# Moving the eight activation homes of a one-core diffusion-step kernel from one phase modulo 512 bytes to eight

## The chip, the cores and the metric

The kernel runs on one core of one Trainium2 chip. The metric is the device time of one execution in microseconds (us). Three executions of the kernel before took 2007.27, 2007.70 and 2008.75 us; the median is 2007.7 us.

## What is computed

One layer of a hybrid backbone runs over 128 context tokens and 256 latent tokens, 384 in all, with a model width of 2048 and a hidden width of 8192, in fp32:

```
mod = SiLU(cond) @ w_ada + b_ada           -> shift1, scale1, gate1, shift2, scale2, gate2
h   = RMSNorm(x)*(1+scale1)+shift1
proj = h @ w_in                            -> gated DeltaNet (8 heads) and mLSTM (4 heads), both directions
x  += gate1 * RMSNorm(concat(heads) @ w_out)
h   = RMSNorm(x)*(1+scale2)+shift2
x  += gate2 * RMSNorm(relu(h @ w_ffn1)^2 @ w_ffn2)
```

Returned are the new x of both token sets and the final states of the context.

## The kernel before

Each large product is made from three products in the one-pass fp32 type (`F32R`). A weight chunk of 256 rows by 512 columns is loaded by SyncE's DMA queue into a tile `raw` (five of them). ScalarE rounds it into `whi` (line 332) and VectorE subtracts to get the remainder `wlo` (line 333), two buffers each. The activations are kept transposed (features on the partitions, 384 tokens along the row) and split the same way into a high and a low part. `gemm` (from line 337) then issues, for each 128 rows of the contraction, three matmuls into one bank:

- feature-major (`fm=True`, lines 356 to 358): the stationary operand is a slice of `whi` or `wlo`, and the moving operand is 384 tokens of an activation tile;
- token-major (`fm=False`, lines 360 to 362): the stationary operand is 128 tokens of an activation tile, and the moving operand is 512 columns of `whi` or `wlo`.

So each of these matmuls reads one activation tile and one weight tile. TensorE loads a stationary operand for each matmul (the profile's PEld), beside the matmul before.

The activation tiles live in eight homes of 128 partitions by 8 x 384 x 4 = 12,288 bytes. Four are in the pool `hp` under the tags `h00`, `h01`, `h10`, `h11` (high and low part of features 0 to 1023 and of 1024 to 2047). They hold the mixer's input `h` (`alloc_act`, line 314), then the mixer's output `y` (line 1259), then the FFN's input `h`, and at the very end four weight tiles (line 1172). Four are in the pool `fp` under the tags `ah` and `al`, two buffers each (lines 1140 and 1141). They hold the squared-ReLU activations of one 1024-wide block of the hidden layer, and for a time also the broadcast gate rows `gp1` and `gp2` (lines 1073 and 1185) and two weight tiles (line 1099).

The stages run in this order: projections for the mLSTM (`phase1`, to about 296 us), mLSTM heads, DeltaNet quarters (`delta_qk`, `delta_v`, `delta_quarter`), output projection (`mid`, to about 925 us) and the FFN (`ffn`: eight rounds of `up`, feature-major, and `down`, token-major, to about 1972 us), then `final`. Small products for `mod` (line 190) are filled in between. The order on each engine is the program's order with priorities; no cost depends on an address. All waits are derived from which instruction reads and writes which part of which tile.

The pools are laid out one behind the other along a partition's row. The first, `cp` (constants), begins with an unused tile `padc` of 88 x 4 = 352 bytes (line 1222); with it, `hp` begins at byte 8,704 = 17 x 512. A home is 24 x 512 bytes, so the four homes of `hp` and the weight pool `wp` behind them all begin at a multiple of 512. The pool `fp` begins with an unused tile of 192 bytes (line 1267) and its large tiles, too, stand at multiples of 512: three tiles `x1`, the four homes and three tiles `y2`, with the small ones behind. A slice of a home starts at a multiple of 1,536 bytes (feature block) or of 512 bytes (128 tokens) inside it, and a slice of `whi` at a multiple of 512, so both operands of every such matmul start at a multiple of 512.

Some other matmul operands stand elsewhere. The split gate weights `wgh` and `wgl` (line 435, one-pass type, 96 columns, rows of 384 bytes) start 224 bytes past a multiple of 512. The mLSTM values `vaug` (line 689, plain fp32, rows of 257 x 4 = 1,028 bytes per head) start at 480, 0 and 32 bytes past one for the three token tiles, and the states `cn` at 192.

Of the kernel before, what the change touches and what calls it, by code (L numbers as in the profile page):

```python
# [12 lines left out]
F32 = mybir.dt.float32  # L13
F32R = mybir.dt.float32r
# [7 lines left out]
P = 128  # L22
# [3 lines left out]
TOK = NT * P  # L26
# [228 lines left out]
def ada_later(S, sec, nvec=0):  # L255

    for i in range(2):
        if i < 2 - nvec:
            S.todo.append(ada_steps(S, [(sec, 1024 * i + 256 * u) for u in range(4)], 256))
        else:  # L260
            S.todo.extend(ada_vec(S, sec, 1024 * i + 512 * h) for h in range(2))


def gate_step(S, i):
    gate_rows(S, i)
    yield
# [44 lines left out]
    return d  # L311


def alloc_act(S):

    hh = [[S.hp.tile([P, 8, TOK], F32R, tag=f"h{a}{b}", name=f"h{a}{b}") for b in range(2)] for a in range(2)]
    return lambda kt: (hh[kt // 8][0][:, kt % 8, :], hh[kt // 8][1][:, kt % 8, :])


# [63 lines left out]
def wcols(w, c0, n=512, kn=2):  # L383
    return lambda kc: [w[kc * kn * P:(kc + 1) * kn * P, c0:c0 + n]]
# [357 lines left out]
def delta_static(S):  # L742
    nc, dl = S.nc, S.dl
    S.Tm = [dl.tile([P, 6, P], F32, name=f"Tm{d}", bufs=1) for d in range(2)]
    S.Nc = dl.tile([P, 6, 64], F32, name="Nc", bufs=1)
    S.tA = dl.tile([P, 13, 32], F32, name="tA", bufs=1)
    S.X = dl.tile([NI, 32, 32], F32, name="X", bufs=1)
    for t in S.Tm + [S.Nc, S.tA]:
        nc.gpsimd.memset(t, 0.0)
# [379 lines left out]
def ffn(S):  # L1129
    nc, tc, A, c = S.nc, S.tc, S.A, S.c  # L1130
    fp = S.fp
    y2 = [fp.tile([P, D], F32, tag=f"y2_{t}", name=f"y2_{t}") for t in range(NT)]
    w1, w2 = A.w_ffn1[0], A.w_ffn2[0]
    NC = FFN // 1024
    psum_dn = lambda s: S.pm.tile([P, 512], F32, tag="m", name="ps_dn")
    act = {}
    gp2 = []

    def up(ch):
        hi = fp.tile([P, 8, TOK], F32R, tag="ah", name="ah", bufs=2)  # L1140
        lo = fp.tile([P, 8, TOK], F32R, tag="al", name="al", bufs=2)

        def evac(s, ps, b):
            i = 4 * b + s
            rl = fp.tile([P, TOK], F32, tag="rl", name="rl", bufs=3)
            nc.scalar.activation(rl, ps[:, 0:TOK], AF.Relu)
            nc.scalar.activation(hi[:, i, :], rl, AF.Square)  # L1147
            nc.gpsimd.tensor_tensor(rl, rl, rl, op=ALU.mult)  # L1148
            nc.vector.tensor_tensor(lo[:, i, :], rl, hi[:, i, :].bitcast(F32), op=ALU.subtract)
        for b in range(2):  # L1150
            gemm(S, True, wcols(w1, ch * 1024 + b * 512), range(8), S.hT, lambda s, ps, b=b: evac(s, ps, b))
        act[ch] = lambda kt: (hi[:, kt, :], lo[:, kt, :])

    ss = fp.tile([P, NT, 4], F32, name="ssf")

    def down(ch):
        def evac(s, ps, n):
            dst = y2[s][:, n * 512:n * 512 + 512]
            if ch == 0:
                nc.scalar.copy(dst, ps)  # L1160
            else:
                nc.vector.tensor_tensor(dst, ps, dst, op=ALU.add)
            if ch == NC - 1:
                junk = fp.tile([P, 512], F32, tag="fj", name="fj", bufs=2)
                nc.scalar.activation(junk, dst, AF.Square, accum_out=ss[:, s, n:n + 1])
                eng = nc.vector if n == 3 else nc.gpsimd
                g = gp2[min(s, 1)][:, n * 512:n * 512 + 512]
                eng.tensor_tensor(g if s != 1 and n == 3 else dst, dst, g, op=ALU.mult)
        for n in range(4):
            room = ()  # L1170
            if ch == NC - 1 and n == 3:
                t = [S.hp.tile([P, 2, 512], F32R, tag=f"h{a}{b}", name=f"w{a}{b}") for a in range(2) for b in range(2)]
                room = [None, None, t[0:2], t[2:4]]
            gemm(S, False, lambda kp, n=n: [w2[ch * 1024 + kp * 256:ch * 1024 + (kp + 1) * 256, n * 512:n * 512 + 512]],
                 range(4), act[ch], lambda s, ps, n=n: evac(s, ps, n), psum_dn, room=room)

    S.rate = 0.0
    up(0)
    S.rate = R3
    for ch in range(NC):  # L1180
        if ch + 1 < NC:
            up(ch + 1)
        if ch == NC - 1:
            for v in range(2):
                g = fp.tile([P, D], F32, tag=("ah", "al")[v], name=f"gp2_{v}", bufs=2)
                nc.sync.dma_start(g, S.gpd[1][v].partition_broadcast(P))
                gp2.append(g)
        down(ch)
    return y2, ss, gp2
# [17 lines left out]
def body(tc, A, O):  # L1207
    with ExitStack() as ctx:
        nc = tc.nc
        S = SimpleNamespace(nc=nc, tc=tc, A=A, O=O, todo=[], credit=0.0, rate=1.7, nraw=5, av=None)  # L1210
        ent = ctx.enter_context
        sub = lambda st, nm, bufs=1: st.enter_context(tc.tile_pool(name=nm, bufs=bufs, reuse_waits="tile"))
        S.cp = ent(tc.tile_pool(name="cp", bufs=1))
        S.hp = ent(tc.tile_pool(name="hp", bufs=1))
        S.wp = ent(tc.tile_pool(name="wp", bufs=2))
        S.wk = ent(tc.tile_pool(name="wk", bufs=2))
        S.dr = ent(tc.tile_pool(name="dr", bufs=2, space=DRAM))
        S.drp = ent(tc.tile_pool(name="drp", bufs=1, space=DRAM))
        S.pg = ent(tc.tile_pool(name="pg", bufs=4, space=PSUM))
        S.pm = ent(tc.tile_pool(name="pm", bufs=3, space=PSUM))  # L1220
        S.pa = ent(tc.tile_pool(name="pa", bufs=1, space=PSUM))
        S.cp.tile([P, 88], F32, name="padc")
        S.gpd = [S.drp.tile([2, D], F32, name=f"gpd{i}") for i in range(2)]
        S.gbd = [S.drp.tile([P, 1024], F32, name=f"gbd{t}") for t in range(NT)]
        with ExitStack() as mx:
            S.gp = sub(mx, "gp")
            S.yB = [S.gp.tile([P, 1024], F32, name=f"yB{t}") for t in range(NT)]
            S.rq, S.ssA, S.fA = [S.gp.tile([P, 8, NT], F32, name=n) for n in ("rq", "ssA", "fA")]
            with ExitStack() as ms:
                S.mp = sub(ms, "mp")  # L1230
                S.ga = sub(ms, "ga")
                with tc.tile_pool(name="p1", bufs=1, reuse_waits="tile") as S.p1:
                    with tc.tile_pool(name="tp", bufs=1, reuse_waits="tile") as S.tp:
                        setup(S)
                    phase1(S)
                S.ml = sub(ms, "ml", 2)
                for h in range(HB):
                    mlstm_head(S, h)
            S.da = sub(mx, "da", 2)
            S.dl = sub(mx, "dl", 2)  # L1240
            S.de = sub(mx, "de", 2)
            S.yA = S.da.tile([P, NT, 1024], F32, name="yA", bufs=1)
            delta_static(S)
            ada_later(S, 2)
            S.todo.append(gate_step(S, 0))
            ada_later(S, 3)
            ada_later(S, 4, ND2)
            ada_later(S, 5, 2)
            S.todo.append(gate_step(S, 1))
            S.rate = R1  # L1250
            rest = None
            for q in range(4):
                prev, rest = rest, delta_quarter(S, q, delta_qk(S, q), delta_v(S, q))
                if prev:
                    prev()
            g0 = ag_block(S, 0)
            rest()
            g1 = ag_block(S, 1)
            yy = [[S.hp.tile([P, 8, TOK], F32R, tag=f"h{a}{b}", name=f"y{a}{b}") for b in range(2)] for a in range(2)]
            S.yT = lambda kt: [yy[1 - kt // 8][b][:, kt % 8, :] for b in range(2)]  # L1260
            for k in range(8):
                split_T(S, [S.yB[t][:, k * P:(k + 1) * P] for t in range(NT)], S.c.nb[:, k % 2:k % 2 + 1], S.yT(8 + k))
            yA_finish(S, 0, g0)
            yA_finish(S, 1, g1)
        S.fp = ent(tc.tile_pool(name="fp", bufs=1, reuse_waits="tile"))
        S.av = S.fp
        S.fp.tile([P, 48], F32, name="padf")
        S.rate = R2
        mid(S)
        S.rate = R3  # L1270
        final(S, *ffn(S))
# [19 lines left out]
```

## Time and profile before

| | |
|---|---|
| median of three executions | 2007.7 us |
| profiled execution | 2004.86 us |
| its span | 2003.1 us |
| TensorE busy | 1944.5 us (97%) |
| VectorE busy | 1166.2 us (58%) |
| ScalarE busy | 711.1 us (35%) |
| granted TensorE clock, mean | 0.991 |

The span is the stretch that the profile covers; 1.8 us of the profiled execution lie outside it. Matmuls are pipelined, so the duration of one (334 ns, say) is longer than the time from its start to the next one's start; it is the latter, called the pitch here, that adds up to the span.

### The profile page before, as it was taken

The numbers are of one execution on the slowest core, as the hardware profiler recorded it, in microseconds if no ns is written. First come the engines' busy times: TensorE is split into PE (matmuls) and PEld (weight loads), VectorE is DVE, ScalarE is ACT, GpSimd is POOL, SyncE is SP. The second block draws the span as 40 slices with busy tenths as digits, with TensorE's granted clock in tenths as the row PEclk, the third lists the DMA queues.
The fourth block names the chain that finished last, engine by engine and source line by source line (L and its number), as shares of the span: only waits on it lengthen the run. The fifth ranks groups of instructions, "written<-read, shape, count | busy, mean of one in ns | idle before, by whom it ended". The sixth has DMA issues, their size and how long they took to land.

```text
span 2003.1 us, 28836 instructions
## 1 busy us (share of the span) xinstructions
PE 1944.5 (97%) x11332; PEld 1673.4 (84%) x11332; DVE 1166.2 (58%) x2144; ACT 711.1 (35%) x1125; POOL 122.8 (6%) x125
## 2 busy tenths in 40 slices
PE   5999997999999999998999999999999999999997
PEld 4677886788888777787998898998989989989886
DVE  3766874668878766767455455556543443343445
ACT  5222243544344334335433342332332423323322
POOL 2000000010000000000100010000000100000002
PEclk9999998999999999998999999999999999999999
DMA  9988438776576566762454554545544344444452
GB/s 271 297 263 261 127 117 167 171 198 192 162 200 188 154 189 201 269 220 64 127 178 158 158 160 147 172 162 158 163 136 130 122 135 126 126 128 127 131 172 105
DMA packets 232356, 337.25 MB, mean 168 GB/s; under 512 B 46272, under 2 KB 115584, under 8 KB 231196
## 3 DMA queue, kind: packets, MB, share of 16 engines
q1 hardware_dynamic: 214120, 333.15, 55.1%
q10 hardware_dynamic: 17620, 2.11, 0.7%
q8 instruction: 89, 1.46, 0.3%
q14 instruction: 47, 0.39, 0.1%
q0 software_dynamic: 480, 0.15, 0.0%
HBM read 326.80 MB, written 8.56 MB: 167 GB/s over the span
## 4 chain that ended last, share of the span: by engine, by line
PE 89%; DMA 5%; DVE 4%; ACT 1%; issue 1%; POOL 0%; SPq 0%; ACTq 0%; DVEq 0%; POOLq 0%
PE ps_g L356 13%; PE ps_g L358 13%; PE ps_g L357 12%; PE ps_dn L360 8%; PE ps_dn L362 8%; PE ps_dn L361 8%; PE ps_g L360 5%; PE ps_g L362 5%; PE ps_g L361 5%; PE ps_ada L190 4%; DMA raw<-w_in 2%; DVE wlo L333 1%; PE ps_o L1027 1%; DMA raw_av<-w_ada 1%; PE ps_num L689 1%
## 5 line engine op out<-in xcount | busy, mean ns | idle before, releaser
L333 DVE TENSOR_TENSOR wlo<-raw,whi 128x1024 fp32r<-128x1024 f32 (+1 forms) x402 | 487.2, 1212 | 568.9 <-ACT whi L332 567.3
L332 ACT CAST whi<-raw 128x1024 fp32r<-128x1024 f32 (+1 forms) x402 | 417.5, 1039 | 1012.3 <-PE ps_g L357 386.8
L356 PE MATMUL ps_g<-h,whi 128*128 128x384 f32 x1536 | 522.8, 340 | 0.6 <-DVE cv L737 0.6
L358 PE MATMUL ps_g<-h,wlo 128*128 128x384 f32 x1536 | 516.3, 337 | 2.1 <-DVE wlo L333 2.1
L357 PE MATMUL ps_g<-h,whi 128*128 128x384 f32 x1536 | 517.0, 337 | 0.0
L356 PEld LDWEIGHTS ps_g<-h,whi 128*128 128x128 f32 x1536 | 288.9, 188 | 20.7 <-issue 18.7
L362 PE MATMUL ps_dn<-wlo,ah 128*128 128x512 f32 x756 | 294.5, 390 | 1.2 <-DVE wlo L333 1.2
L360 PE MATMUL ps_dn<-whi,al 128*128 128x512 f32 x756 | 294.8, 390 | 0.0
L361 PE MATMUL ps_dn<-whi,ah 128*128 128x512 f32 x756 | 294.5, 390 | 0.0
L358 PEld LDWEIGHTS ps_g<-h,wlo 128*128 128x128 f32 x1536 | 288.6, 188 | 5.1 <-DVE wlo L333 3.6
L357 PEld LDWEIGHTS ps_g<-h,whi 128*128 128x128 f32 x1536 | 288.9, 188 | 1.2 <-issue 0.7
L362 PEld LDWEIGHTS ps_dn<-wlo,ah 128*128 128x128 f32 x756 | 141.9, 188 | 31.5 <-DVE wlo L333 2.0
L360 PEld LDWEIGHTS ps_dn<-whi,al 128*128 128x128 f32 x756 | 141.9, 188 | 31.0 <-issue 1.6
L361 PEld LDWEIGHTS ps_dn<-whi,ah 128*128 128x128 f32 x756 | 141.9, 188 | 29.0
L220 DVE SCALAR_TENSOR_TENSOR adav<-raw_av,scz,adav 128x512 f32<-128x512 f32 x180 | 130.4, 773 | 12.3 <-DMA raw_av<-w_ada 12.3
L1148 POOL TENSOR_TENSOR rl<-rl 128x384 f32<-128x384 f32 x64 | 68.0, 1070 | 876.2 <-ACT ah L1147 876.0
L360 PE MATMUL ps_g<-whi,h 128*128 128x512 f32 x288 | 119.1, 413 | 1.3 <-ACT whi L332 1.2
L361 PE MATMUL ps_g<-whi,h 128*128 128x512 f32 x288 | 115.2, 400 | 0.0
L362 PE MATMUL ps_g<-wlo,h 128*128 128x512 f32 x288 | 114.2, 400 | 0.2 <-DVE wlo L333 0.2
L190 PE MATMUL ps_ada<-raw_ada,scz 128*32 128x256 f32 (+1 forms) x1216 | 100.6, 387 | 4.0 <-DMA raw_ada<-w_ada 2.6
L360 PEld LDWEIGHTS ps_g<-whi,h 128*128 128x128 f32 x288 | 54.5, 189 | 24.2 <-issue 11.7
L190 PEld LDWEIGHTS ps_ada<-raw_ada,scz 128*32 128x32 f32 x1216 | 33.9, 113 | 46.4 <-issue 27.2
(400 smaller groups left out, 1895.5 us busy)
## 6 DMA issues: line engine op xcount, KB each, us to landing
raw<-w_ffn SPq DMA_DIRECT2D x256, 512.0 KB, 3.8
raw_ada<-w_ada SPq DMA_DIRECT2D x80, 512.0 KB, 4.8
raw<-w_in SPq DMA_DIRECT2D x74, 512.0 KB, 4.7
raw_ada<-w_ada SPq DMA_DIRECT2D x128, 256.0 KB, 4.5
raw_av<-w_ada SPq DMA_DIRECT2D x48, 512.0 KB, 4.3
raw<-w_in SPq DMA_DIRECT2D x76, 256.0 KB, 3.1
raw<-w_out SPq DMA_DIRECT2D x32, 512.0 KB, 4.5
x<-x_sample SPq DMA_DIRECT2D x2, 1024.0 KB, 10.3
```

What stands on the lines that cost most here:

```text
L190: nc.tensor.matmul(ps[32 * j:32 * j + 32, 0:n], lhsT=c.scz[:, k + kk, :], rhs=raw[:, kk, u * n:u * n + n], start=k + kk < npar, stop=k + k ...
L220: nc.vector.scalar_tensor_tensor(acc[:, v, :], in0=raw[:, kt % 2, :], scalar=w, in1=acc[:, v, :], op0=ALU.mult, op1=ALU.add)
L332: nc.scalar.copy(hi, raw)
L333: nc.vector.tensor_tensor(lo, raw, hi.bitcast(F32), op=ALU.subtract)
L356: nc.tensor.matmul(o, lhsT=hi[:, kk, w], rhs=al, start=st, stop=False)
L357: nc.tensor.matmul(o, lhsT=hi[:, kk, w], rhs=ah, start=False, stop=False)
L358: nc.tensor.matmul(o, lhsT=lo[:, kk, w], rhs=ah, start=False, stop=sp)
L360: nc.tensor.matmul(o, lhsT=al[:, w], rhs=hi[:, kk, :], start=st, stop=False)
L361: nc.tensor.matmul(o, lhsT=ah[:, w], rhs=hi[:, kk, :], start=False, stop=False)
L362: nc.tensor.matmul(o, lhsT=ah[:, w], rhs=lo[:, kk, :], start=False, stop=sp)
L689: nc.tensor.matmul(o, lhsT=l, rhs=r, start=n == 0, stop=n == len(ops) - 1)
L1148: nc.gpsimd.tensor_tensor(rl, rl, rl, op=ALU.mult)
```

## The change

Each home gets 16 more fp32 elements (64 bytes) at its end, through a helper `act_tile` that allocates a flat tile and hands out a view of its first 8 x 384 elements in the shape of before. The unused tile at the start of `cp` shrinks from 352 to 96 bytes. So `cp`'s tiles and the first home move down by 256 bytes. The four homes of `hp` begin at 256, 320, 384 and 448 modulo 512. `wp` and what follows keep their places. The four homes of `fp` begin at 0, 64, 128 and 192, and what stands behind them in `fp` (`y2`, `adav`, `rl` and small tiles) moves up by 256 bytes. No instruction is added or removed, and none changes its shape.

```diff
+def act_tile(pool, tag, name, bufs=1):
+
+    t = pool.tile([P, 8 * TOK + 16], F32R, tag=tag, name=name, bufs=bufs)
+    return t[:, 0:8 * TOK].rearrange("p (k n) -> p k n", k=8)
+
+
 def alloc_act(S):
 
-    hh = [[S.hp.tile([P, 8, TOK], F32R, tag=f"h{a}{b}", name=f"h{a}{b}") for b in range(2)] for a in range(2)]
+    hh = [[act_tile(S.hp, f"h{a}{b}", f"h{a}{b}") for b in range(2)] for a in range(2)]
...
-        hi = fp.tile([P, 8, TOK], F32R, tag="ah", name="ah", bufs=2)
-        lo = fp.tile([P, 8, TOK], F32R, tag="al", name="al", bufs=2)
+        hi = act_tile(fp, "ah", "ah", 2)
+        lo = act_tile(fp, "al", "al", 2)
...
-        S.cp.tile([P, 88], F32, name="padc")
+        S.cp.tile([P, 24], F32, name="padc")
...
-            yy = [[S.hp.tile([P, 8, TOK], F32R, tag=f"h{a}{b}", name=f"y{a}{b}") for b in range(2)] for a in range(2)]
+            yy = [[act_tile(S.hp, f"h{a}{b}", f"y{a}{b}") for b in range(2)] for a in range(2)]
```

## Rows read from the trace of the kernel before

**Rows 1.** The page: busy time by engine, then the chain of waits by engine.
```profile
PE 1944.5 (97%) x11332; PEld 1673.4 (84%) x11332; DVE 1166.2 (58%) x2144; ACT 711.1 (35%) x1125; POOL 122.8 (6%) x125
...
PE 89%; DMA 5%; DVE 4%; ACT 1%; issue 1%; POOL 0%; SPq 0%; ACTq 0%; DVEq 0%; POOLq 0%
```

**Rows 2.** Windows: stretch, length, busy PE, PEld, DVE, ACT, POOL, clock, DMA.
```profile
1100.00:1972.00 872.00, 870.12 (x4399) 785.61 (x4398) 411.17 (x455) 277.64 (x331) 60.58 (x54) 1.00 0.47 144
```

**Rows 3.** Groups by line: shapes, count, busy us, mean ns, idle before.
```profile
L356 PE MATMUL ps_g<-h,whi 128*128 128x384 f32 x1536 | 522.8, 340 | 0.6 <-DVE cv L737 0.6
...
L362 PE MATMUL ps_dn<-wlo,ah 128*128 128x512 f32 x756 | 294.5, 390 | 1.2 <-DVE wlo L333 1.2
...
L360 PE MATMUL ps_g<-whi,h 128*128 128x512 f32 x288 | 119.1, 413 | 1.3 <-ACT whi L332 1.2
...
L360 PE MATMUL ps_g<-whi,y 128*128 128x512 f32 x180 | 71.3, 396 | 0.0
```

**Rows 4.** Timeline of a feature-major stretch, first and last of 23 matmuls.
```profile
1400.10 0.33 PE L356 MATMUL ps_g<-h,whi 128*128 128x384 f32 x1
...
1403.91 0.33 PE L357 MATMUL ps_g<-h,whi 128*128 128x384 f32 x1
```

**Rows 5.** Timeline of a token-major stretch, first and last of 19 matmuls.
```profile
1469.71 0.39 PE L362 MATMUL ps_dn<-wlo,ah 128*128 128x512 f32 x1
...
1473.79 0.39 PE L362 MATMUL ps_dn<-wlo,ah 128*128 128x512 f32 x1
```

**Rows 6.** Timeline, gate products of feature blocks 14 and 15, eight matmuls.
```profile
259.93 0.51 PE L435 MATMUL ps_gates<-h,wgh 128*96 128x384 f32 x2
...
260.45 0.34 PE L356 MATMUL ps_g<-h,whi 128*128 128x384 f32 x1
...
260.62 0.51 PE L435 MATMUL ps_gates<-h,wgh 128*96 128x384 f32 x2
...
261.15 0.34 PE L357 MATMUL ps_g<-h,whi 128*128 128x384 f32 x1
```

**Rows 7.** Timeline, mLSTM products of head 0, first and last of five pairs.
```profile
311.64 0.60 PE L689 MATMUL ps_num<-vaug,E 128*128 128x257 f32 x2
...
313.37 0.60 PE L689 MATMUL ps_num<-vaug,E 128*128 128x257 f32 x2
```

**Rows 8.** Groups by line: ScalarE and VectorE results in homes and elsewhere.
```profile
L1162 DVE TENSOR_TENSOR y<-ps_dn,y 128x512 f32<-128x512 f32 x84 | 57.8, 688 | 21.6 <-PE ps_dn L362 20.7
...
L1147 ACT ACTIVATE ah<-rl 128x384 fp32r<-128x384 f32 x64 | 33.7, 526 | 2.0
...
L417 DVE TENSOR_TENSOR vaug<-ps_g,vaug 128x512 f32<-128x512 f32 x48 | 32.0, 686 | 13.6 <-PE ps_g L362 13.4
...
L739 ACT ACTIVATE slq<-cv 128x384 f32<-128x384 f32 x16 | 7.5, 516 | 5.0 <-DVE cv L737 4.9
```

**Rows 9.** DMA issues (median us to landing), then one tile's instructions with first starts.
```profile
gp<-gpd SPq DMA_DIRECT2D x8, 256.0 KB, 4.2
...
gp<-gpd SPq DMA_DIRECT2D x2, 1024.0 KB, 8.0
...
L1081 DVE TENSOR_TENSOR x<-ps_g,gp x12: 679/684/693, 809.8 to 913.9; 128x512 f32<-128x512 f32 x12
L1168 POOL TENSOR_TENSOR y<-y,gp x9: 1286/1293/2279, 1942.6 to 1977.8; 128x512 f32<-128x512 f32 x9
L1087 SPq DMA_DIRECT2D gp<-gpd x8: 339/460/1425, 778.0 to 819.0; - x8
L1186 SPq DMA_DIRECT2D gp<-gpd x2: 344/356/367, 1926.4 to 1926.9; - x2
```

**Rows 10.** Timeline at the FFN's start: its first matmul, a later split.
```profile
924.99 0.42 PE L356 MATMUL ps_g<-h,whi 128*128 128x384 f32 x1
...
934.52 0.55 DVE L304 TENSOR_TENSOR h<-hfull,h 128x384 fp32r<-128x384 f32 x1
```

## The prediction

> **What bounds the kernel now.** I read the page's busy times first, then the chain of waits, then the groups by line, and last the timeline of single matmuls. TensorE is busy 97% of the span, and 89% of the chain that ended last is TensorE's own work [rows 1]. In the FFN's windows it is tighter: of 872 us TensorE is busy 870.1, at a granted clock of 1.00, which is the level of 2.4 GHz [rows 2]. So nothing that hides beside TensorE moves the end there; only the time from one matmul's start to the next one's does.
>
> Reading that pitch: 23 feature-major matmuls start between 1400.10 and 1403.91 us, so 3.81 / 22 = 173.2 ns each [rows 4]. 19 token-major ones start between 1469.71 and 1473.79 us, 4.08 / 18 = 226.7 ns each [rows 5]. The difference of 53.5 ns for 128 more columns is 0.418 ns a column, one column per cycle at 2.4 GHz. What is left is the same for both: 173.2 - 384/2.4 = 13.2 ns and 226.7 - 512/2.4 = 13.3 ns. Each matmul of the one-pass type thus pays about 13.3 ns beside its columns. Every one of them reads an activation home and a weight tile, both at a multiple of 512 bytes.
>
> How many there are: line 356 has 1536, as have 357 and 358; lines 360 to 362 have 756, 288 and 180 each in the three groups shown [rows 3]. That is 3 x 1536 + 3 x (756 + 288 + 180) = 8,280. Their pitch alone is 4,608 x 0.1732 + 3,672 x 0.2267 = 1,631 us of the span. One nanosecond more or less on each is 8.3 us. This is the number that decides the case.
>
> **The change part by part.** It adds and removes no instruction, no wait and no transfer. Four things could still have a price.
>
> *TensorE reading a home at another phase.* The trace of before has no matmul of the one-pass type that moves an operand from another phase, so I bound it by two neighbours. First, the gate products move the same homes, but their stationary weights start at 480 and 352 bytes modulo 512 in the two blocks shown, not even at a multiple of 64. From 259.93 to 261.15 us there are seven pitches, six of gate matmuls and one of line 356 between: 1.22 us, or 174.3 ns [rows 6]. Seven pitches with all operands at 0 are 7 x 173.2 = 1.212 us. The difference is 1.1 ns a matmul, and readings in steps of 0.01 us leave 1.4 ns either way: -0.3 to +2.5 ns. Over 8,280 matmuls that is -2.5 to +20.7 us. Second, the mLSTM products move rows that start at 480, 192, 0 and 32: ten matmuls of 257 columns in pairs, of which the first and the last pair stand in the rows, and from pair to pair 1.73 / 4 = 432.5 ns, 216.3 ns each [rows 7]. These take two cycles a column (514 / 2.4 = 214.2 ns) and keep 2.1 ns beside, so a moving operand at any of these phases costs nothing to be seen there. The first neighbour has the right pace and the wrong operand, the second the right operand and half the pace. I take 0, since both lie within their resolution of it, and keep the ends for the range.
>
> *ScalarE and VectorE writing homes at another phase.* ScalarE writes 384 elements into `ah`, at 0, in 526 ns, and into `slq`, which does not stand at a multiple of 512, in 516 ns. VectorE adds 512 elements into `vaug` in 686 ns and into `y2`, at 0, in 688 ns [rows 8]. So -10 to +10 ns per instruction. Even 10 ns on `ah`'s 64 would be 0.6 us of an engine that is idle for two thirds of the span [rows 1]. Value 0; cover: TensorE's matmuls.
>
> *Gate rows landing in homes at another phase.* The broadcast rows for the output projection come in eight transfers from 778.0 us on, each landing in 4.2 us, and are first read at 809.8 us; the two of the FFN are issued at 1926.4 us, land in 8.0 us and are first read at 1942.6 us [rows 9]. The second pair has some 16.2 - 8.0 = 8 us in hand, so a transfer of double length would just be hidden. Value 0. If the cover went, one transfer's length of 8 us would be the most.
>
> *Tiles that move along.* `cp`'s constants, `y2`, `adav` and `rl` shift by 256 bytes. They keep their phase modulo 256; the equal 686 and 688 ns above speak for 0. The new end of `fp` makes one of the residual tiles share bytes with other tiles of the DeltaNet pool than before. These have been read for the last time before the output projection starts, so the wait is over before it is asked for.
>
> The sum is 0 against the profiled execution's 2004.86 us, which lies 2.8 us below the median of the three executions; the forecast is made on the median: 2007.7 us.
>
> By the rule of the Trainium skill, "TensorE: Matmul & The Clock Gate", section "Back-to-back issue gap", a warm matmul needs N/2.4 + 2.5 ns, which is 162.5 and 215.8 ns here. The trace differs: 173.2 and 226.7. If the homes' common phase caused the difference of 10.8 ns, the estimate by that page would be 8,280 x 0.0108 = 89 us less, 1918 us; the rival below is priced from rows alone.
>
> **The rivals.**
>
> *Slower: a home's start off the multiple of 512 costs TensorE part of a cycle group.* Place: each of the 8,280 matmuls, at its first columns. Price: 1.1 ns each, from the gate rows, 9.1 us: 2016.8 us; at their upper end, 2.5 ns, 2028.4 us. It decides from 0.5 ns on, which is 4 us. For it: the seven gate pitches are not shorter but, if anything, longer. Against it: these follow a change of stationary shape, and the mLSTM rows show nothing.
>
> *Faster: the 13.3 ns are a collision.* The load of the next stationary operand runs beside the matmul, and both start at phase 0, so they could meet in the same part of the memory each time. With the phases apart, the remainder could fall to what the mLSTM matmuls show, 2.1 ns: 8,280 x 11.2 = 92.7 us, 1915 us. If it helps only in part, by a tenth, it is 9 us: 1998.4 us. For it: the fixed remainder is six times that of the fp32 matmuls. Against it: the gate weights are already apart from the homes, and nothing of the 13.3 ns is gone there; and the remainder does not vary with what VectorE and ScalarE do at the time.
>
> *Slower: waits by whole homes.* If the flat tile's view were followed as one piece, the FFN's first matmul, at 924.99 us, which needs block 0 alone, would wait for the split of block 7, which begins at 934.52 us and takes 0.55 [rows 10]: 10.1 us there, 2017.8 us, and more in the first stage, where blocks are split as they are used. Against it: slices of views are used all over this program.
>
> *The change doesn't do what it says.* If the allocator rounds the homes up to 512 bytes, all phases stay equal: 2007.7 us, as in the forecast.
>
> **How the numbers follow.** A change of 0.2%, 4 us, is about what a measurement of this kernel tells from none. The forecast has 0.70, with the unmoved homes at 0.03 beside it, so "same" is 0.73. The slower start has 0.13 and the waits by whole homes 0.03: "slower" 0.16. The collision has 0.11, of which I give the large gain 0.04: "faster" 0.11. The likeliest is 2007.7 us. Its own range is 2003.7 to 2011.7. To leave out no more than 2 in 10, the range reaches up over both slower rivals at their middle prices and down to the lower bound from the gate rows, -2.5 us, with the measurement's 4 us: 2001 to 2020 us. The upper ends, 2028 us and the large gain, stay outside.
>
> **What would show it.** Right: in the same stretches of the FFN the pitches are 173.2 and 226.7 ns again, TensorE is busy 870 of 872 us, and line 1147 takes 526 ns. The slower start: a longer pitch in one of the two forms, most likely the feature-major one, in which the home streams. If only token-major ones grow, it is the stationary side. The collision: a pitch nearer 163 and 216 ns, in every stage. Waits by homes: idle time of TensorE that VectorE's line 304 ends, near 925 us. The prediction is wrong if a pitch moves by over 0.5 ns, or if the schedule's order changes although no cost depends on an address.

## The result and the profile after

The changed kernel takes 2028.3 us, the median of three executions (2023.7 to 2030.8), against 2007.7 before: a ratio of 1.0098, with a 95% interval of 1.0069 to 1.0127. It is slower by 1.0%, and the forecast of no change was wrong. The profiled execution took 2023.71 us with a span of 2022.0, which is 18.9 us more than the span of before. All lines of the code past the new helper stand six further down: 356 to 358 are now 362 to 364, and 360 to 362 are now 366 to 368.

The page of after, busy time by engine and the chain of waits by engine, answers to [rows 1]:

```profile
PE 1965.9 (97%) x11332; PEld 1680.7 (83%) x11332; DVE 1167.2 (58%) x2144; ACT 712.1 (35%) x1125; POOL 122.7 (6%) x125
...
PE 87%; DMA 6%; DVE 5%; ACT 1%; issue 1%; POOL 0%; SPq 0%; ACTq 0%; DVEq 0%; POOLq 0%
```

The same 11,332 matmuls keep TensorE busy 21.4 us longer; the other three engines grew by no more than 1.0 us. The window over the FFN (stretch, length, busy time and instructions of PE, PEld, DVE, ACT and POOL, granted clock, DMA share) answers to [rows 2]:

```profile
1100.00:1972.00 872.00, 870.36 (x4349) 779.71 (x4348) 403.46 (x448) 272.37 (x322) 55.63 (x51) 1.00 0.47 142
```

This row is the whole case. TensorE is as full as before (870.4 of 872 us) and its granted clock is 1.00 as before, the level of 2.4 GHz. But it got through 4,349 matmuls where it had got through 4,399. One matmul costs 870.36 / 4,349 = 200.1 ns here, and cost 870.12 / 4,399 = 197.8 ns before: no wait has appeared, the matmuls are slower. Where a stretch is this full, the count beside the busy time is the first thing to compare.

Which of them are slower is read from the timeline. First a feature-major stretch of after, the first and the last of 23 matmuls, which answers to [rows 4], then a token-major one, the first and the last of 19, which answers to [rows 5]:

```profile
1469.50 0.34 PE L362 MATMUL ps_g<-h,whi 128*128 128x384 f32 x1
...
1473.36 0.34 PE L363 MATMUL ps_g<-h,whi 128*128 128x384 f32 x1
```

```profile
1399.79 0.40 PE L367 MATMUL ps_dn<-whi,ah 128*128 128x512 f32 x1
...
1403.95 0.39 PE L367 MATMUL ps_dn<-whi,ah 128*128 128x512 f32 x1
```

The pitches are 3.86 / 22 = 175.5 ns and 4.16 / 18 = 231.1 ns, against 173.2 and 226.7. The durations of the single matmuls (0.34 and 0.39 to 0.40 us) hardly show it, because they overlap; the starts do.

Over the whole trace I took the time from each such matmul's start to the next one's, kept the pairs of one form that follow each other without a gap (no longer than 1.15 times the columns' time with 13.3 ns), and averaged them. "FFN second product" is the one into `ps_dn`, which reads the homes in `fp`; "other token-major" are those on `h` and `y`, in the homes of `hp`. The last two rows each count in 36 matmuls whose weight tile stands in a home; the prediction's 8,280 leaves these 72 out.

| form | matmuls | before, ns | after, ns | more, us |
|---|---|---|---|---|
| feature-major | 4,608 | 173.71 | 174.85 | 5.3 |
| FFN second product | 2,304 | 226.92 | 231.13 | 9.7 |
| other token-major | 1,440 | 228.43 | 231.89 | 5.0 |

The last column is the count times the difference. It adds up to 20.0 us, beside 18.9 us between the two spans and 20.6 us between the medians. So the pitch is enough to account for the loss, if all of it reaches the end. The FFN's first matmul starts 5.5 us later than in [rows 10]:

```profile
930.53 0.42 PE L362 MATMUL ps_g<-h,whi 128*128 128x384 f32 x1
```

From there to the end of the span the loss is 18.9 - 5.5 = 13.4 us. The FFN's share of the table is 9.7 for its second product and 3,072 x 1.14 ns = 3.5 for its first, together 13.2 us. For this part the account closes. The 5.5 us ahead of it say less: in four kernels of the experiments that keep the pitches of before (e6, e2, e8 and e1), the FFN starts at 928.8, 931.8, 934.1 and 939.2 us in the one execution that was profiled, and in a second trace of the changed kernel (e7) at 936.0.

The writes into the homes took what they took before, as the groups by line show (count, busy us, mean ns, idle time before); the first two answer to [rows 8], the third to [rows 3], and the last to line 361 of before, which had 294.5 us and 390 ns:

```profile
L1168 DVE TENSOR_TENSOR y<-ps_dn,y 128x512 f32<-128x512 f32 x84 | 57.9, 689 | 23.8 <-PE ps_dn L368 21.6
...
L1153 ACT ACTIVATE ah<-rl 128x384 fp32r<-128x384 f32 x64 | 33.7, 527 | 2.0
...
L362 PE MATMUL ps_g<-h,whi 128*128 128x384 f32 x1536 | 525.9, 342 | 0.0
...
L367 PE MATMUL ps_dn<-whi,ah 128*128 128x512 f32 x756 | 298.6, 395 | 0.0
```

ScalarE's write into `ah` has a mean of 527 ns (526 before), and VectorE's into `y` 689 (688). The gate rows of the FFN, which answer to [rows 9], land in 8.5 us and are read 16.5 us after they are issued, so they stay hidden:

```profile
gp<-gpd SPq DMA_DIRECT2D x2, 1024.0 KB, 8.5
...
L1174 POOL TENSOR_TENSOR y<-y,gp x9: 1293/1302/2282, 1960.8 to 1996.6; 128x512 f32<-128x512 f32 x9
L1192 SPq DMA_DIRECT2D gp<-gpd x2: 345/350/355, 1944.3 to 1944.8; - x2
```

### The profile page after: what moved, and what is told of

The parts are those of the page before. It is cut to its first block, busy times and chain, and to the rows that moved or that the text cites. A ratio compares the mean times of both kernels' runs of the same rounds, so it can differ in the third digit from the quotient of the medians.

```text
span 2022.0 us, 28837 instructions
## 1 busy us (share of the span) xinstructions
PE 1965.9 (97%) x11332; PEld 1680.7 (83%) x11332; DVE 1167.2 (58%) x2144; ACT 712.1 (35%) x1125; POOL 122.7 (6%) x125
## 4 chain that ended last, share of the span: by engine, by line
PE 87%; DMA 6%; DVE 5%; ACT 1%; issue 1%; POOL 0%; SPq 0%; ACTq 0%; DVEq 0%; POOLq 0%
PE ps_g L362 13%; PE ps_g L364 13%; PE ps_g L363 13%; PE ps_dn L367 9%; PE ps_dn L366 9%; PE ps_dn L368 9%; PE ps_g L366 4%; PE ps_g L368 4%; PE ps_g L367 4%; PE ps_ada L190 3%; DMA raw<-w_in 3%; DVE wlo L339 2%; PE ps_o L1033 1%; PE ps_num L695 1%; ACT whi L338 1%
## 5 line engine op out<-in xcount | busy, mean ns | idle before, releaser
L338 ACT CAST whi<-raw 128x1024 fp32r<-128x1024 f32 (+1 forms) x402 | 417.7, 1039 | 1025.8 <-PE ps_g L363 392.1
L362 PEld LDWEIGHTS ps_g<-h,whi 128*128 128x128 f32 x1536 | 289.0, 188 | 20.2 <-issue 18.5
L367 PE MATMUL ps_dn<-whi,ah 128*128 128x512 f32 x756 | 298.6, 395 | 0.0
L368 PE MATMUL ps_g<-wlo,y 128*128 128x512 f32 x180 | 71.7, 398 | 0.8 <-DVE wlo L339 0.6
## 6 DMA issues: line engine op xcount, KB each, us to landing
x<-x_sample SPq DMA_DIRECT2D x2, 1024.0 KB, 10.1
```

Source lines behind the costliest of these rows:

```text
L338: nc.scalar.copy(hi, raw)
L362: nc.tensor.matmul(o, lhsT=hi[:, kk, w], rhs=al, start=st, stop=False)
L367: nc.tensor.matmul(o, lhsT=ah[:, w], rhs=hi[:, kk, :], start=False, stop=False)
L368: nc.tensor.matmul(o, lhsT=ah[:, w], rhs=lo[:, kk, :], start=False, stop=sp)
```

## The experiments

The theory to test, A: what sets the pitch is where the moving and the stationary operand of these matmuls start relative to each other, modulo some power of two; it is best when the two are equal, as all were before. The rivals: that each operand's own distance from a multiple of 512 bytes costs, whatever the other one does; and that the loss comes from something beside the two operands. An account that came up later, that the 13.3 ns left at equal phases could be got rid of too, has its own run. The expectations stand as they were written ahead of each run. Ratios are against the kernel before on the same chip in the same session, where its median was 2012.3 to 2013.3 us.

**Single matmuls at every phase (m1_phases).** This kernel leaves the whole layer out. TensorE issues 24 one-pass matmuls after each other from one pair of addresses, then from the next pair; beside it VectorE copies one column per pair, and no other engine computes.

```diff
+for s in range(0, 512, 64):
+    for m in range(0, 512, 64):
+        BLOCKS.append((f"A512 s{s} m{m}", [(s, m, 512)]))
...
+                nc.tensor.matmul(ps[:, 0:w], lhsT=st[:, s // 4:s // 4 + P], rhs=mv[:, m // 4:m // 4 + w],
```

> This kernel leaves the whole layer out. It issues only one-pass fp32 matmuls, 24 in a row for each pair of operand addresses: stationary operand s bytes and moving operand m bytes past a multiple of 512, for all 8 x 8 multiples of 64, then steps of 4 bytes, other widths, and the kernel's own order of three products. No other engine works beside it. Theory A (the stationary load of the next matmul and the moving stream of this one meet in the memory, and what counts is the difference of their phases): the pitch at 512 columns is a function of (s - m) modulo 512 alone; equal phases give 226.7 ns, and some differences give 222 to 236 ns. Theory B (an operand that doesn't start at a multiple of 512 costs by itself): 226.7 ns at s = m = 0 only, more on every other row and column of the table, also where s = m. Theory C (what got slower was the company of the other engines, not the addresses): 226.7 ns everywhere, within 0.5.

Six rows of its timeline, each 21 matmuls of 512 columns in a stretch of one pair (start, length, then the count at the end). The (stationary, moving) starts are (4096, 0), (0, 64), (0, 128), (0, 192), (64, 0) and (64, 64):

```profile
634.53 4.92 PE L66 MATMUL ps<-mv,st 128*128 128x512 f32 x21
...
24.25 4.97 PE L66 MATMUL ps<-mv,st 128*128 128x512 f32 x21
...
29.77 5.04 PE L66 MATMUL ps<-mv,st 128*128 128x512 f32 x21
...
35.35 5.06 PE L66 MATMUL ps<-mv,st 128*128 128x512 f32 x21
...
63.10 5.06 PE L66 MATMUL ps<-mv,st 128*128 128x512 f32 x21
...
68.70 4.93 PE L66 MATMUL ps<-mv,st 128*128 128x512 f32 x21
```

Each length is 20 pitches and one matmul's duration of 0.39 us: (4.92 - 0.39) / 20 = 226.5 ns in the first row, 233.5 in the fourth and fifth. Two things are to be seen. The last row has both operands 64 bytes off and is as good as the first to 0.01 us in 20 pitches. And (0, 64) and (64, 0) differ, 4.97 against 5.06: the sign counts.

All 64 pairs of the table fall into four classes by (moving - stationary) modulo 256 bytes, 16 pairs in each (at 512 columns, the mean of the last twelve pitches of each pair; the very first pair, in which the clock rises, is left out):

| moving - stationary | 0 | 64 | 128 | 192 |
|---|---|---|---|---|
| 512 columns, ns | 226.7 | 228.8 to 228.9 | 232.4 to 233.3 | 233.3 |
| 384 columns, moving at 0, ns | 173.3 | 173.4 | 176.0 | 176.7 |

Adding 512 to 32,768 bytes to the stationary side gives 226.7 ns each time. The order of the kernel's own three matmuls, at its addresses (`ah` at 64, `al` at 128), was tried as well, together with the same at (0, 0); 70 and 69 matmuls of the two:

```profile
685.13 16.34 PE L66 MATMUL ps<-mv,st 128*128 128x512 f32 x70
...
656.29 15.80 PE L66 MATMUL ps<-mv,st 128*128 128x512 f32 x69
```

(16.34 - 0.39) / 69 = 231.2 ns and (15.80 - 0.39) / 68 = 226.6 ns, where the changed kernel's second product shows 231.13 and the kernel before 226.92. So a stream of matmuls with no other engine at work but that copy reproduces the loss. A holds for starts at multiples of 64 and 512 columns, with a period of 256 bytes; that something beside the two operands does it is refuted, and so, by the first and the last of the six rows, is the distance from a multiple of 512. One thing is not explained by the four classes: in that order the three pitches are 229.0, 236.0 and 228.3 ns, a mean of 231.1, where the classes of the three pairs give 232.4 to 233.3 for each. So the order of the products enters the pitch, and the kernel shows the same pattern: in three of the FFN's rounds (the second, fourth and sixth) its three pitches are 229.1 to 229.4, 235.7 to 235.9 and 228.3 to 228.4 ns. The mixer's homes, run in the same way at (256, 320) and (384, 448), give 231.1 and 233.1 ns token-major and 173.8 and 175.6 ns feature-major. The means, 232.1 and 174.7, lie within 0.3 ns of what the changed kernel shows for these forms.

**Everything off by 64 (e1_all_by_64).** The same question in the whole kernel: all tiles behind the constants, homes and weights, start 64 bytes past a multiple of 512.

```diff
-        S.cp.tile([P, 88], F32, name="padc")
+        S.cp.tile([P, 104], F32, name="padc")
```

> The kernel before with 64 more bytes in the unused first tile, so that homes, weight tiles and the FFN's tiles all begin at 64 modulo 512: no operand of the one-pass matmuls starts at a multiple of 512, but all have one phase. Theory A (difference of phases): pitches of 173.2 and 226.7 ns as before and 2007.7 us, within 4. Theory B (a start off the multiple of 512): slower by 10 us or more, 2018 to 2030 us. Theory C (company of the other engines): 2007.7 us.

The window over the FFN:

```profile
1100.00:1972.00 872.00, 870.12 (x4399) 785.79 (x4398) 406.14 (x451) 275.10 (x325) 55.81 (x51) 1.00 0.47 144
```

4,399 matmuls in 870.12 us, the very numbers of before, and the pitches are 173.71, 226.92 and 228.42 ns. A start off the multiple costs the matmuls nothing as long as both operands are off alike. The time is 2016.8 against 2013.3 us, a ratio of 1.0021 (1.0010 to 1.0032): some 4 us came from elsewhere, which the last experiment follows up.

**Finer phases, other widths, other types (m2_fine).** Also without the layer. It asks whether some start beats the common phase, and what kind of matmul is affected.

```diff
+for x in range(0, 256, 4):
+    BLOCKS.append((f"N512 m{x}", "r", 128, [(0, x, 512)]))
+    BLOCKS.append((f"N384 m{x}", "r", 128, [(0, x, 384)]))
+for rows in (32, 64, 96, 128):
+    for x in (0, 64, 128, 192):
+        BLOCKS.append((f"rows{rows} m{x}", "r", rows, [(0, x, 512)]))
+for ty in "bf":
+    for x in range(0, 256, 32):
+        BLOCKS.append((f"type {ty} m{x}", ty, 128, [(0, x, 512)]))
```

> The layer is left out again; 20 one-pass fp32 matmuls in a row for each moving start from 0 to 252 bytes in steps of 4 (512 and 384 columns, stationary operand at 0), then stationary operands of 32 to 128 columns, then bf16 and plain fp32 operands at eight moving starts. Theory A1 (the load of 128 stationary columns takes its 13.3 ns out of the moving stream, and a wrong phase adds to it): no start gives less than 226.7 and 173.3 ns; narrower loads leave less beside the columns, about 13.3 x columns / 128. Theory A2 (the 13.3 ns are a fixed pause): the same remainder of 13.3 ns for all widths of load. Theory A3 (the 13.3 ns are themselves a collision that some phase avoids): some start gives clearly less, down to 216 ns. For bf16 and plain fp32, which read at most half as much per ns, all three expect no dependence on the start, within 1 ns.

Its timeline, 17 matmuls each: one-pass with the moving operand at 0 and at 72, one-pass with a stationary operand of only 32 columns, bf16, and plain fp32 at 32 (where each matmul is two passes, one behind the other, and the row counts the passes):

```profile
22.75 4.02 PE L71 MATMUL ps<-mv,st 128*128 128x512 f32 x17
...
169.61 4.16 PE L71 MATMUL ps<-mv,st 128*128 128x512 f32 x17
...
546.13 4.10 PE L71 MATMUL ps<-mv,st 128*32 128x512 f32 x17
...
620.20 3.83 PE L71 MATMUL ps<-mb,sb 128*128 128x512 bf16 x17
...
673.83 7.46 PE L71 MATMUL ps<-mf,sf 128*128 128x512 f32 x17
```

Of the 64 starts none gave less than 226.7 ns at 512 columns or 173.3 at 384; the worst were 240.0 and 180.7. Many of the means lie on 226.7, 233.3 and 240.0, which are steps of 6.7 ns, 16 cycles at 2.4 GHz; the others lie between. So the pitch of before is the floor, and the hope of a better layout than "all equal" falls. A narrower stationary load does not help: with 32 columns of it the pitch is 231.7 ns at 0, more than with 128. So the price does not grow with the size of the load (A1), nor is it the same for all widths (A2). bf16 takes 215.8 ns a matmul and plain fp32 429.2 a pass, 858 a matmul, at all eight starts tried (a few bf16 records are missing from the trace, where one gap is twice as long): these two do not see the phase at all.

The difference of the starts is not the whole rule. Two rows with 384 columns and a difference of 192, the first from m1_phases with (stationary, moving) at (64, 0), the second from m2_fine at (0, 192):

```profile
544.29 3.52 PE L66 MATMUL ps<-mv,st 128*128 128x384 f32 x19
...
419.19 3.11 PE L71 MATMUL ps<-mv,st 128*128 128x384 f32 x17
```

The pitches are 176.7 and 173.3 ns. At 512 columns and starts between the multiples of 64 equal differences part too: 232.5 ns at (4, 0) and 226.7 at (0, 252). What holds in every case tried with 128 stationary columns and 384 or 512 moving ones is that nothing beats the equal start.

**Homes at 0 and 256 (e2_steps_of_256).** The homes alternate between 0 and 256 bytes modulo 512, in `hp` (with the unused tile of `cp` at 24 elements) and, with the same helper, in `fp`.

```diff
+def act_tile(pool, tag, name, bufs=1, more=64):
...
-    hh = [[S.hp.tile([P, 8, TOK], F32R, tag=f"h{a}{b}", name=f"h{a}{b}") for b in range(2)] for a in range(2)]
+    hh = [[act_tile(S.hp, f"h{a}{b}", f"h{a}{b}", 1, 64 * (a + b == 0)) for b in range(2)] for a in range(2)]
```

> As the changed kernel, but a home steps by 256 bytes instead of 64: the two buffers of the FFN's high part stand at 0 and 256, those of the low part at 0 and 256, one of the mixer's four homes at 256 and the other three at 0 modulo 512. Theory A (the pitch follows the difference of phases modulo 256, as the table of the isolated matmuls has it): every difference is 0 modulo 256, pitches of 173.2 and 226.7 ns, and the time of before within 0.3%. Theory D (any home that stands elsewhere than the others modulo 512 costs): token-major pitches of the FFN of 229 ns or more, and at least 0.4% slower.

```profile
1100.00:1972.00 872.00, 870.12 (x4399) 785.71 (x4398) 409.07 (x454) 277.17 (x331) 60.65 (x54) 1.00 0.47 144
```

In the FFN's window nothing has moved, and the time is 2014.1 against 2013.1 us, ratio 1.0010 (0.9998 to 1.0022). In the whole kernel too the period is 256 bytes, and having unequal starts modulo 512 is no cost in itself. Nor is the helper: the flat tile and its view are those of the change.

**All homes half a period off (e3_all_homes_128).** Homes at 384 modulo 512, weights at 0: a case worse than the change, with all homes alike.

```diff
+    S.fp.tile([P, 96], F32, name="padh")
...
-        S.cp.tile([P, 88], F32, name="padc")
+        S.cp.tile([P, 56], F32, name="padc")
+        S.wp.tile([P, 32], F32, name="padw", bufs=1)
```

> All eight homes at 384 modulo 512 (128 modulo 256), weight tiles at 0 as before: the homes have one phase among themselves, but another than the weights. Theory A, from the table of isolated matmuls: token-major pitch 232.4 to 233.3 ns (5.7 to 6.6 more, 3,744 matmuls, 21 to 25 us) and feature-major pitch 176.0 ns (2.7 more, 4,608 matmuls, 12 us): 33 to 37 us slower, 1.7 to 1.8%. Theory D (the homes must stand alike among themselves): as before, within 0.3%.

```profile
1100.00:1972.00 872.00, 870.53 (x4324) 778.23 (x4323) 400.45 (x446) 270.55 (x321) 53.35 (x51) 1.00 0.46 141
```

Only 4,324 matmuls in the window, 201.3 ns each. The pitches are 175.93, 232.66 and 232.32 ns, which by the counts of the table above make 10.2 + 13.2 + 5.6 = 29.0 us. Measured were 2036.9 against 2013.1 us, ratio 1.0114 (1.0091 to 1.0137), or 24 us. The direction and the token-major pitch came as expected, the total was set too high: the feature-major pitch grew by 2.2 ns and not by the 2.7 of the single matmuls, and a part of the growth did not reach the end. It is not the stepping of the homes that costs, but their distance from the weights.

**The FFN's homes alone, and the mixer's alone (e4_ffn_homes_only, e5_mixer_homes_only).** The change in two halves, with its helper: first only `ah` and `al` in `fp`, then only the `h` and `y` homes in `hp` (the line for `y` is changed like that for `h`).

```diff
-        hi = fp.tile([P, 8, TOK], F32R, tag="ah", name="ah", bufs=2)
-        lo = fp.tile([P, 8, TOK], F32R, tag="al", name="al", bufs=2)
+        hi = act_tile(fp, "ah", "ah", 2)
+        lo = act_tile(fp, "al", "al", 2)
```

> Half of the change: only the FFN's four homes step by 64 (0, 64, 128, 192 modulo 512); the mixer's four stay at 0. Theory A: the token-major pitch of the FFN's second product rises by what the changed kernel showed, 4.2 ns on 2,268 matmuls, 9.6 us (0.48%); feature-major 173.2 ns as before. Theory D and any account by the order of work: the loss can't be split by homes; all or nothing of the 1%.

```diff
-    hh = [[S.hp.tile([P, 8, TOK], F32R, tag=f"h{a}{b}", name=f"h{a}{b}") for b in range(2)] for a in range(2)]
+    hh = [[act_tile(S.hp, f"h{a}{b}", f"h{a}{b}") for b in range(2)] for a in range(2)]
...
-        S.cp.tile([P, 88], F32, name="padc")
+        S.cp.tile([P, 24], F32, name="padc")
```

> The other half: only the mixer's four homes step by 64 (256 to 448 modulo 512); the FFN's four stay at 0. Theory A: feature-major pitch up by about 1.1 ns on 4,300 (4.9 us) and the token-major pitches that read h and y up by 4 ns on some 1,000 (4.2 us): 9.1 us, 0.45%; the FFN's second product at 226.7 ns as before. The two halves add up to the changed kernel's 0.9 to 1.0%.

The FFN's window, first of the kernel with the FFN's homes stepped, then of the one with the mixer's:

```profile
1100.00:1972.00 872.00, 870.18 (x4362) 779.52 (x4361) 404.63 (x450) 271.96 (x323) 55.84 (x51) 1.00 0.47 143
```

```profile
1100.00:1972.00 872.00, 870.30 (x4387) 786.65 (x4386) 405.20 (x449) 274.94 (x325) 55.64 (x51) 1.00 0.47 144
```

Of the 50 matmuls lost in this window, 37 go with the FFN's homes and 12 with the mixer's, whose last use, `h` of the FFN, falls into it. Each half moves only the forms that read its homes: 231.14 ns in the second product in the one, 174.86 (feature-major) and 232.05 (other token-major) in the other, all else as before. The first half costs 9.9 us, ratio 1.0046 (1.0033 to 1.0059), where the pitch predicts 10.1. The second costs 4.7 us, ratio 1.0026 (1.0016 to 1.0037), 3.2 to 7.4 us, where the pitch predicts 10.5. So some of the mixer's longer pitch does not reach the end. In the FFN it does, as the time from the FFN's first matmul to the end of the span shows. It is 1,078.2 to 1,078.4 us in the five traces with the old pitches (before, e1, e2, e6, e8). It is 9.4 us longer than before with the FFN's homes stepped (9.8 by pitch and count), 3.8 with the mixer's (3.5), 13.3 and 13.7 in the two traces of the change (13.2) and 19.9 in e3 (20.0). That leaves, of the second half's 4.7 us, about 1 us for the stages ahead of the FFN, where the pitch makes 7.0. These stages are less full (in the first 296 us of the changed kernel TensorE is busy 275.4), so a slower matmul may there take the place of a wait. Which waits gave way is not shown: single executions differ by up to 14 us at the FFN's start without any change of pitch.

**Everything off by 256 (e6_all_by_256), and the change once more (e7_changed_again).** The first is e1 with 256 bytes for 64 (the unused tile has 24 elements), the second the changed kernel itself, on the same chip as the two halves.

```diff
-        S.cp.tile([P, 88], F32, name="padc")
+        S.cp.tile([P, 24], F32, name="padc")
```

> The kernel before with 256 bytes fewer in the unused first tile: everything behind it moves by 256 bytes, all tiles of the one-pass matmuls at 256 modulo 512, none of their differences changed. Theory A: pitches and time of before, within 0.1%. It is set beside the shift by 64, which took 0.2% more at unchanged pitches: if that came from transfers that land off a multiple of 256, this one shows nothing; if any shift of the constants costs, it shows 0.2% as well.

> The changed kernel, timed beside its halves on one chip. Theory A: 0.9 to 1.0% slower than before, the sum of the halves, with the token-major pitch of the FFN's second product at 231 ns on average and the feature-major at 174.8.

The FFN's window of the first, then of the second:

```profile
1100.00:1972.00 872.00, 870.12 (x4399) 785.69 (x4398) 409.31 (x454) 276.86 (x331) 60.61 (x54) 1.00 0.47 144
```

```profile
1100.00:1972.00 872.00, 870.37 (x4348) 780.24 (x4347) 402.70 (x447) 272.42 (x323) 55.67 (x51) 1.00 0.46 142
```

Moved by 256 the kernel is the kernel before: 2012.4 against 2012.3 us, ratio 0.9996 (0.9987 to 1.0006). The change itself gave 2029.2 us, ratio 1.0079 (1.0066 to 1.0092), and its pitches came back to within 0.01 ns in the first two forms and 0.12 in the third. The halves add up to 0.46 + 0.26 = 0.72%, beside 0.79%. These 17 us, with an interval of 13.3 to 18.5, are less than the 20 us of the pitch: the FFN's 13.2 us are in them whole, the other 6.8 in part.

**Only the load tiles off by 64 (e8_raw_by_64).** Where do e1's 4 us come from, if not from the matmuls? Here the tiles `raw` alone, into which the weight chunks are loaded, start 64 bytes past a multiple of 256; homes and split weights stand at multiples of it.

```diff
+    if not hasattr(S, "padw"):
+        S.padw = S.wp.tile([P, 48], F32, name="padw", bufs=1)
...
-        S.cp.tile([P, 88], F32, name="padc")
+        S.cp.tile([P, 24], F32, name="padc")
+        S.wp.tile([P, 16], F32, name="padr", bufs=1)
```

> Only the five load tiles raw stand 64 bytes past a multiple of 256; the mixer's homes stand at 256 modulo 512, the FFN's homes and the weight tiles at 0, so no phase between the operands of the one-pass matmuls changes. If the 0.2% of the shift by 64 came from transfers that land off a multiple of 256 bytes, this one is 0.2% slower as well, with longer landings in the first 300 us; if not, it is as before within 0.1%. Theory A: the pitches are 173.2 and 226.7 ns in either case.

The time is 2017.7 against 2013.2 us, ratio 1.0027 (1.0014 to 1.0040), with the pitches of before (173.72, 226.93, 228.35). So e1's loss goes with where `raw` starts. Its readers are not slower (ScalarE's rounding of it has a mean of 1036 ns, 1039 before), and the loads of `w_ffn` and `w_in`, which took 3.8, 4.7 and 3.1 us before, land within 0.1 us of that:

```profile
raw<-w_ffn SPq DMA_DIRECT2D x256, 512.0 KB, 3.8
raw<-w_in SPq DMA_DIRECT2D x74, 512.0 KB, 4.6
...
raw<-w_in SPq DMA_DIRECT2D x76, 256.0 KB, 3.2
raw<-w_out SPq DMA_DIRECT2D x32, 512.0 KB, 5.0
```

Those of `w_out` took 5.0 us, and 4.5 before, but they took 4.9 in e6 as well, which lost nothing. So the longer landings that were expected do not show. In the traces of e1 and e8 the time from the FFN's first matmul on is that of before (1,078.4 and 1,078.3 against 1,078.2 us), so the 4 us arise ahead of it; how, stays open. It has no part in the result, since the change leaves `raw` where it was.

## Why the prediction was wrong

The step that failed is the first of the four: "*TensorE reading a home at another phase*". It was bounded by -0.3 and +2.5 ns a matmul and taken as 0, "since both lie within their resolution of it". It measured +1.14 ns on 4,608 feature-major matmuls, +4.21 on 2,304 of the FFN's second product and +3.46 on the other 1,440: 20.0 us, 2.4 ns on average. The average lies just under the upper bound; the token-major forms lie beyond it. The bound itself, +20.7 us over all matmuls, would have let the measured time in, but the range was drawn at the middle price and ended at 2020 us.

*Why the neighbours did not bound it.* What counts is how the two operands start relative to each other, in a matmul of the one-pass type. The mLSTM products [rows 7] had the difference but are plain fp32, and m2_fine shows plain fp32 at 429.2 ns a pass at every start: they could not have shown anything. The gate products [rows 6] were the right type with a difference, and their +1.1 ns was of the size that the feature-major form then showed, +1.14; I rated it as less than the reading's own 1.4 ns. That the two agree so closely is chance: the gate products' starts lie 32 and 160 bytes apart modulo 256, the homes' 0, 64, 128 and 192, and m2_fine has 173.3 to 180.7 ns at 384 columns. And they are feature-major and 96 columns wide on the stationary side, and nothing in the trace of before had a token-major matmul of this type with unequal starts. For that form there was no neighbour at all, and the range should have been left open there. The bound was taken over from one form to the other because the floor of 13.3 ns was common to both.

*The rival on the slower side* had the right sign, and its upper end, 2028.4 us, came within 0.2 us of the measured median. That is luck, since 2.5 ns was the edge of a reading and no measured price. Its mechanism is refuted: it put the price on each start's distance from a multiple of 512, and e1 moves every operand off by 64 without changing one pitch.

*The rival on the faster side* had the right place and the wrong sign. The stationary and the moving operand do affect each other through where they start; that the load of the next stationary operand meets the stream is a reading of this which no run here shows by itself. But equal phases are the best case, not the collision: no start in m2_fine goes below 226.7 or 173.3 ns. The 13.3 ns belong to the one-pass type. The Trainium skill, "TensorE: Matmul & The Clock Gate", section "Back-to-back issue gap", gives a warm matmul taken by itself N/2.4 + 2.5 ns, 215.8 at 512 columns, and for a stream of weight loads and matmuls about 131 ns. In m2_fine, which is such a stream, bf16 takes 215.8 ns, the first figure to the digit; the one-pass type takes more at any phase, and the second figure is not seen.

Another rule of the Trainium skill speaks for the forecast, and the measurement decides against it. The Trainium skill, "SBUF — State Buffer", section "Who interferes with whom", gives TensorE one read port for the moving operand and an independent one for the weight load, and knows of contention only at the port that VectorE and GpSimd share. Here the two reads are not independent: 226.7 to 233.3 ns by their relative start alone, with no other engine reading.

*The other two rivals.* No wait by whole homes appeared. The FFN's first matmul starts at 930.53 us, 9.5 us ahead of the split of block 7, which answers to the second of [rows 10]:

```profile
940.04 0.55 DVE L304 TENSOR_TENSOR h<-hfull,h 128x384 fp32r<-128x384 f32 x1
```

And the change does what it says: each half of it moves the pitches of the forms that read its homes and no others, while e6 and e2, in which phases stay equal modulo 256, keep the old pitches.

*The other terms held.* ScalarE's and VectorE's writes moved by 1 ns, the gate rows stayed hidden, and the tiles that move along cost nothing (e6 moves all of them by 256 for a ratio of 0.9996). The 11,332 matmuls start in the same order in both traces, but for four pairs of small 32 x 32 products whose two members change places. The part on what would show it was of use with its 0.5 ns, the point at which the prediction falls. It was wrong on the form: it held the feature-major pitch most likely to grow, and the token-major ones grew three to four times as much. Nor is a token-major loss the mark of the stationary side, as it said: (0, 192) and (64, 0) cost the same in m1_phases.

## What to carry to other kernels

Where TensorE is full, let both operands of one-pass fp32 matmuls with 128 stationary and 384 or 512 moving columns start at the same place modulo 256 bytes (tried at multiples of 64): unequal starts cost up to 6.7 ns of a 226.7 ns matmul at multiples of 64, here 0.8 to 1.0% of the kernel, while bf16 and plain fp32 don't care. To find such a loss, compare the number of matmuls in an equally full window and the times between their starts, since busy shares and single durations hide it. And a neighbour in the trace bounds a cost only if it has the same type, the same form and the changed property at once; where there is none, leave the range open.

## What was not expected of the hardware

- The pitch of one-pass fp32 matmuls with 512 columns, at starts that are multiples of 64, depends on (moving - stationary) modulo 256 bytes: 226.7, 228.9, 232.4 to 233.3 and 233.3 ns for 0, 64, 128 and 192. At starts between it goes up to 240.0, and equal differences no longer give equal pitches. At 384 columns 64 costs nothing (173.4 ns), and 192 costs 3.3 ns at (64, 0) and nothing at (0, 192).
- At 128 columns the phase does not matter: 111.6 to 111.8 ns at all eight starts tried, and at 256 columns the equal start is the worst of them by 2 ns (119.7 against 117.8).
- A stationary operand of 32 columns made the matmul slower, 231.7 against 226.7 ns at equal starts. With 64 and 96 columns the equal start is not the best: 230.0 ns for both, against 228.3 with the moving operand at 64 bytes (64 columns) and at 192 bytes (96 columns).
- Load tiles that start 64 bytes past a multiple of 256 cost this kernel 0.27% (0.14 to 0.40) without any longer median transfer or reader.
